# Reordering products in a Strassen feed-forward block: P2 behind the last pair's P4, another start, and P2 second in the second product

## The chip, the core and the metric

The kernel runs on one NeuronCore of one Trainium2 chip. The metric is device time in microseconds (us). A run is one launch of the whole kernel; the figure for a kernel is the median of its runs. TensorE (PE in the profile) multiplies matrices into PSUM, VectorE (DVE), ScalarE (ACT) and GpSimd (POOL) do the elementwise work, and SyncE (SP) issues the DMA transfers.

## What is computed

One decoder block on a sequence of 1024 tokens of width 1024, in float32. The change touches only the second half, the feed-forward part with 2 x 2816 hidden columns:

```python
def conv_ffn(h, w_up, conv_w, conv_b, w_down):
    u = causal_dwconv(h @ w_up, conv_w) + conv_b
    gate, val = jnp.split(u, 2, axis=-1)
    return (jax.nn.silu(gate) * val) @ w_down

x = layer_norm(ALPHA * x + (1.0 + gt_a) * y, ln1_g[l], ln1_b[l])
h = x * (1.0 + sc_f) + sh_f
y = conv_ffn(h, ffn_w_up[l], ffn_conv[l], ffn_conv_b[l], ffn_w_down[l])
x = layer_norm(ALPHA * x + (1.0 + gt_f) * y, ln2_g[l], ln2_b[l])
```

## The kernel before

**Precision.** Every float32 matrix is held as a high part and a rest ("hi" and "lo", in the names aH/aL, whi/wlo, vh/vl, s1l), and every block product is three matmuls: hi x lo, lo x hi, hi x hi.

**The first product, h @ w_up (lines 1281 to 1535).** It is a Strassen-Winograd scheme: the operands are split 2 x 2 (tokens and reduction on one side; reduction, and gate or value columns, on the other), and seven products P1 to P7 replace eight. The 2816 gate columns go in 22 blocks of 128, each with its block of value columns; one such block f is called a pair here. `product(f, i)` issues Pi of pair f: 12 matmuls of 128x512 at line 1281. A pair owns two PSUM tiles of two halves each: gp[f] holds P2 in half 0 and collects P1, P6, P7, P4 in half 1; vp[f] holds P5 and then P3 in half 0. Dependencies are tracked by whole tiles, so a matmul into one half waits for a reader of the other.

`carry(f, i)` does what must follow a product. After P1 ScalarE copies half 1 (L1471, the p1 copy), after P5 it copies vp (L1473), after P6 it copies the running sum (L1475). `add_p1` (L1458, VectorE) adds the p1 copy to P2's half. After P3 VectorE adds at L1479, after P7 at L1481. Then `conv` makes the causal convolution of 1024 tokens (ScalarE at L1400, two VectorE operations at L1403), first for the value block after P7, then for the gate block after P4, where silu (L1462) and the multiplication by the value block (L1463) follow. The sums that the second product needs are made and split at L1410 and L1411 and stored to DRAM buffers dS1 to dS7 (L1412, L1413, L1427, L1434) two pairs at a time.

`weights(f + 1)` makes the sums of weight blocks for the next pair on VectorE while a pair runs: L1333 (which waits for the weight load vq, issued at L1326), L1336, L1346, L1347, each split at L1305 and L1306. L157 and L158 split the raw weight block.

The order of TensorE's work is written out by hand (`manual_schedule`); the other engines' orders are made by a scheduler from the program text. Before, a pair runs as P2(f), P4(f-1), P6(f), P3(f), P7(f), P1(f+1), P5(f+1). The last pair has P4(f-1), P6, P3, P7, P2 and then P4.

**Where the first product begins (lines 1288 to 1385).** The last layer-norm rows are transposed (`h2_of(t)`), and sums of the left operand (s1 to s4, L1363) are made by VectorE while the first products run.

**The second product, (silu(gate) x val) @ w_down (lines 1545 to 1720).** Again seven products, each of 11 steps j with 4 row blocks t: 132 matmuls (L1634 to L1636). `ORDER` sets the order of the products; P4 comes last, row block by row block, its last one in two column halves. `entry(i, j)` loads an operand pair five steps ahead of TensorE into a ring of eight slots (L1611 to L1620): the left operand from dS, the right one from w_down, through `b_of`, which keeps some blocks in R0 and R1 and others in a ring of six buffers "bt". Two sets of PSUM banks take turns: on1 collects P1, P6, P7, P4; on5 takes P5, P3, P2. `collect` adds a finished product to the accumulators, and `ln2` normalises a row block and stores it. All loads are issued by SP in one queue.

Of the kernel before, what the change touches and what calls it, by code (L numbers as in the profile page):

```python
# [87 lines left out]
def build(ctx, tc, out, cst, x, c, ln0_g, ln0_b, w_ada, b_ada, w_in, dn_conv, dn_a_log, dn_dt_bias,  # L88
# [1198 lines left out]
    with tc.manual_schedule(engines={PE.engine}):  # L1287
        for t in range(NT):
            y_half(t, 1)
            ln1(t)  # L1290
            if t >= LAG:
                h2_of(t - LAG)
        raw = {0: gate_block(0), 1: gate_block(1)}
        product(0, 1)
        product(0, 2)
    mix.close()
    ffn1 = ExitStack()
    fp = ffn1.enter_context(tc.tile_pool(name="ffn1", bufs=1, reuse_waits="tile"))
# [66 lines left out]
    with tc.manual_schedule(engines={PE.engine}):  # L1365
        load_w(0)
        ahead = weights(0)
        next(ahead)
        next(ahead)
        h2_of(NT - 2)  # L1370
        product(1, 1)
        next(ahead)
        for i, tag in ((5, "s1"), (6, "s2"), (3, "s4"), (7, "s3")):
            hi = {5: aH[:, KH[0], HS[1]], 7: aL[:, KH[0], HS[1]]}.get(i)
            if hi is None:
                hi = ft([P, 4, 512], tag + "h", 1, F32R)
            parts_s[i] = hi, ft([P, 4, 512], tag + "l", 1, F32R)
            opA[i] = (lambda k, hl=parts_s[i]: tuple(a[:, :, ct(k)] for a in hl))
        h2_of(NT - 1)
        product(1, 2)  # L1380
        for i in (5, 6):
            for r0, r1 in ((0, 2), (2, 3), (3, 4)):
                split_last = s_rows(i, r0, r1)
        next(ahead, None)
        for i, rows in ((3, ((0, 4),)), (7, ((0, 3), (3, 4)))):
            for r0, r1 in rows:
                with tc.issue_after(split_last[0].ins), tc.issue_after(split_last[1].ins):
                    s_rows(i, r0, r1)
# [49 lines left out]
    def residual_rows(n):  # L1438

        hf, t = n // NT, n % NT  # L1440
        if t == 0:
            for box, v, tag in ((g1h, ln1_g, "g1h"), (b1h, ln1_b, "b1h")):
                box[0] = ft([P, 512], tag, 1)
                nc.sync.dma_start(box[0], v[0][HS[hf]].partition_broadcast(P))
                S.mul(box[0], box[0], ALPHA)
        r = r_cells[n % 2]
        d = ax2[t * P:(t + 1) * P, HS[hf]]
        nc.sync.dma_start(r, d)
        yield
        with tc.issue_after(anchor[0].ins):  # L1450
            V.tensor_tensor(r, r, g1h[0], op=ALU.mult)
            V.tensor_tensor(r, r, b1h[0], op=ALU.add)
        nc.sync.dma_start(d, r)

    pending, anchor = [], [None]

    def add_p1(f):
        V.tensor_tensor(gp[f][:, 0, :], gp[f][:, 0, :], p1_, op=ALU.add)  # L1458
# [8 lines left out]
    def carry(f, i):  # L1467

        g, v = gp[f], vp.get(f)
        if i == 1:  # L1470
            S.copy(p1_, g[:, 1, :])  # L1471
        elif i == 5:
            S.copy(p5_, v[:, 0, :])  # L1473
        elif i == 6:
            S.copy(u2_, g[:, 1, :])  # L1475
        elif i == 2 and f < NF - 1:
            add_p1(f)
        elif i == 3:
            anchor[0] = V.tensor_tensor(v[:, 0, :], v[:, 0, :], u2_, op=ALU.add)  # L1479
        elif i == 7:  # L1480
            V.tensor_tensor(v[:, 1, :], g[:, 1, :], p5_, op=ALU.add)  # L1481
            if f == 0:
                V.tensor_tensor(g[:, 1, :], g[:, 1, :], p4_, op=ALU.add)
            conv(g_row(f), NF + f, v)
            if f == 0:
                gate_end(f)
        elif i == 4 and f:
            if f == NF - 1:
                add_p1(f)
            gate_end(f)  # L1490
# [8 lines left out]
    with tc.manual_schedule(engines={PE.engine}):  # L1499
        product(0, 4)  # L1500
        S.copy(p4_, vp[0][:, 1, :])
        for f, i in ((0, 1), (0, 2), (1, 1), (1, 2)):
            carry(f, i)
        load_w(1)
        ahead = weights(1)
        next(ahead)
        for i in (5, 6, 3, 7):
            step(0, i)
            if i != 5:
                next(ahead, None)  # L1510
        for f in range(1, NF):
            more = f + 1 < NF
            if f == 1:
                seq = (5, 6, 3, 7)
            elif more:
                seq = (2, -4, 6, 3, 7)
            else:
                seq = (-4, 6, 3, 7, 2)
            if more:
                load_w(f + 1)  # L1520
                ahead = weights(f + 1)
            for i in seq:
                step(*((f, i) if i > 0 else (f - 1, -i)))
                if i == (5 if f == 1 else -4):
                    split_q(f, 4, wq[f])
                    if more:
                        next(ahead)
                    if 4 <= f < 4 + 2 * NT:
                        pending.append(residual_rows(f - 4))
                elif i in (6, 3, 7) and more:  # L1530
                    next(ahead, None)
            if more:
                step(f + 1, 1)
                step(f + 1, 5)
        step(NF - 1, 4)
        while pending:
            for _ in pending.pop(0):
                pass
# [18 lines left out]
    ln2_rows = []  # L1557
    stat2 = dt_([P, NT, 4, 6], "stat2")
    R0 = fr.tile([P, NJ, 512], F32, tag="R0", name="R0")
    ORDER = (1, 5, 6, 3, 7, 2, 4)  # L1560
    SPARE = (NJ - 3, NJ - 2, NJ - 1)
    ents, spare2 = {}, []
    R1_ = []
# [4 lines left out]
    def b_of(i, j):  # L1568

        r0, r1 = R0[:, j, :], R1_[0][:, j, :] if R1_ else None  # L1570
        if i in (6, 3):
            b = dt_([P, 512], "bt", 6)
            load_b(b, j, 1, 1)
            if i == 3:
                return b
            V.tensor_tensor(r1, b, r1, op=ALU.subtract)
            return r1
        if i == 1:
            load_b(r0, j, 0, 0)
        elif i == 2:  # L1580
            load_b(r0, j, 1, 0)
        elif i == 5:
            load_b(r1, j, 0, 1)
            V.tensor_tensor(r1, r1, r0, op=ALU.subtract)
            return r1
        elif i == 7:
            V.tensor_tensor(r0, r1, r0, op=ALU.subtract)
        else:
            V.tensor_tensor(r0, r0, r1, op=ALU.subtract)
        return r0  # L1590

# [83 lines left out]
    def collect(i, t, pb):  # L1675
        if i == 1:
            S.copy(c11(t), pb)
        elif i == 5:
            S.copy(c22(t), pb)
        elif i == 6:  # L1680
            S.copy(c12(t), pb)
        elif i == 3:
            done(c12(t), pb, HS[1], res[t, 1], c12(t))
            stats(t, HS[1], 512)
        elif i == 7:
            done(c22(t), pb, HS[1], res[t + 4, 1], c22(t))
            stats(t + 4, HS[1], 512 if t < 3 else 256)
        elif i == 2:
            done(c11(t), pb, HS[0], res[t, 0], c11(t))
            stats(t, HS[0], 512)  # L1690
            ln2(t, 2, CUT_EARLY)

    steps = [(i, j) for i in ORDER for j in range(NJ)]
    AHEAD = 5
    with tc.manual_schedule(engines={PE.engine}):
        n = AHEAD
        for s in steps[:AHEAD]:
            entry(*s)
        nc.sync.dma_start(gate, dG5.partition_broadcast(P))
        two = lambda: [b[:, h, :] for b in (bank2(0), bank2(1)) for h in range(2)]  # L1700
        on1, on5 = two(), two()
        for i in ORDER[:-1]:
            pbs = on5 if i in (5, 3, 2) else on1
            for j in range(NJ):
                if n < len(steps):
                    entry(*steps[n])
                    n += 1
                if i == 3 and j == 0:
                    ln2_rows.extend(rows_of(2, ln2_g[0], ln2_b[0]))
                if j == 4:  # L1710
                    for t in range(4):
                        if i in (3, 7, 2):
                            residual(t + 4 if i == 7 else t, 0 if i == 2 else 1)
                for t in range(4):
                    matmuls(pbs[t], i, j, t)
            for t in range(4):
                collect(i, t, pbs[t])
        while n < len(steps):
            entry(*steps[n])
            n += 1  # L1720
        for t in range(4):
            residual(t + 4, 0)
        for t in (0, 2, 1, 3):
            for sl in (HS[0],) if t < 3 else (slice(0, 256), slice(256, 512)):
                for j in range(NJ):
                    matmuls(on1[t][:, sl], 4, j, t, sl)
                done(acc[:, t + 4, sl], on1[t][:, sl], sl, res[t + 4, 0][:, sl])
                stats(t + 4, sl, 512 if t < 3 else 256)
            ln2(t + 4, 2 if t < 3 else 4, CUT_EARLY if t < 3 else CUT)
# [21 lines left out]
```

## Time and profile before

| | us |
|---|---|
| median of 3 runs (1445.4 to 1447.4) | 1446.18 |
| the profiled execution's own time | 1447.39 |
| its span in the profile | 1445.7 |

Busy over the span, from the page: PE 1337.2 us (92%), DVE 1005.0 (70%), ACT 590.1 (41%), POOL 532.9 (37%). The first product runs from about 745 to 1215 us of the span, the second from there to the end.

The page gives the totals; the trace behind it can be asked for a stretch of time. A windows view gives busy time, granted TensorE clock (1.00 is full speed) and DMA share by stretch; a waits view sums the time an engine sat idle, by the line that waited and what released it; a timeline gives single instructions, with the idle time before each in brackets; a lines view groups instructions by line and shape.

### The profile page before, as it was taken

What the parts mean: (1) busy time and instruction counts of PE and PEld (TensorE: products, weight loads), DVE (VectorE), ACT (ScalarE), POOL (GpSimd) and SP (SyncE); (2) the same over time, 40 slices, a digit from 0 to 9 for tenths busy, and PEclk for the clock granted to TensorE, in tenths of its full rate; (3) what the DMA queues carried; (4) which work ended last, traced back from release to release, by engine and by line L of the source; (5) the groups of instructions that cost most, each with busy time, mean ns of one, the idle gap of its engine ahead of it and who ended that gap; (6) DMA issues with size and microseconds to landing.
All of it is one profiled execution on the core that took longest, in us unless ns stands there. A gap on an engine that the chain in (4) does not pass through costs nothing.

```text
span 1445.7 us, 19012 instructions
## 1 busy us (share of the span) xinstructions
PE 1337.2 (92%) x6662; PEld 1061.9 (73%) x6662; DVE 1005.0 (70%) x1770; ACT 590.1 (41%) x957; POOL 532.9 (37%) x369
## 2 busy tenths in 40 slices
PE   6796999999999899999988989999899998999995
PEld 4564768787887678777866767777687786788885
DVE  7885955487547432794497768877988887732777
ACT  4356222233234332352565444454544544353222
POOL 2674311122115667352323433444444331342006
PEclk9898999999999999899999999999999998999998
DMA  9557212122203464253132343445444438975773
GB/s 316 148 157 208 65 32 59 32 68 57 58 23 102 139 190 146 88 189 117 78 113 80 103 140 126 143 160 189 148 143 160 153 119 307 391 243 162 266 252 117
DMA packets 195572, 209.15 MB, mean 145 GB/s; under 512 B 30099, under 2 KB 125199, under 8 KB 195477
## 3 DMA queue, kind: packets, MB, share of 16 engines
q1 hardware_dynamic: 195189, 206.89, 44.5%
q8 instruction: 53, 0.87, 0.3%
q10 hardware_dynamic: 288, 1.05, 0.2%
q14 instruction: 42, 0.34, 0.1%
HBM read 149.92 MB, written 57.97 MB: 144 GB/s over the span
## 4 chain that ended last, share of the span: by engine, by line
PE 50%; DVE 23%; DMA 10%; issue 9%; POOL 4%; ACT 3%; SPq 1%; POOLq 0%; DVEq 0%; ACTq 0%
PE up L1281 9%; PE pp L622 6%; PE pp L623 5%; PE pp L624 5%; PE up L1634 4%; PE up L1636 4%; PE up L1635 4%; DMA vq<-in_ffn_w_up 3%; DVE ob L1403 2%; DVE vq L1333 1%; POOL vl L1306 1%; PE dn L864 1%; DVE mac L236 1%; DMA K<-in_w_ada 1%; DVE vl L1306 1%
## 5 line engine op out<-in xcount | busy, mean ns | idle before, releaser
L622 PE MATMUL pp<-aH,wlo 128*128 128x512 f32 x432 | 190.9, 442 | 8.8 <-DVE ob L651 6.4
L158 POOL TENSOR_TENSOR wlo<-wst,whi 128x1024 fp32r<-128x1024 f32 x50 | 122.6, 2452 | 160.0 <-ACT whi L157 159.5
L624 PE MATMUL pp<-aH,whi 128*128 128x512 f32 x432 | 176.8, 409 | 0.0
L623 PE MATMUL pp<-aL,whi 128*128 128x512 f32 x432 | 176.7, 409 | 0.0
L1306 POOL TENSOR_TENSOR vl<-vq,vh 128x512 fp32r<-128x512 f32 x44 | 70.2, 1595 | 213.3 <-ACT vh L1305 209.0
L1634 PE MATMUL up<-aL,aH 128*128 128x512 f32 (+1 forms) x304 | 118.7, 391 | 11.8 <-DVE ob L1669 7.1
L1403 DVE SCALAR_TENSOR_TENSOR ob<-up,colC,ob 128x1023 f32<-128x1023 f32 (+1 forms) x88 | 112.2, 1276 | 20.8 <-ACT ob L1400 19.5
L1635 PE MATMUL up<-aH,aL 128*128 128x512 f32 (+1 forms) x304 | 118.2, 389 | 0.0
L1636 PE MATMUL up<-aH 128*128 128x512 f32 (+1 forms) x304 | 118.2, 389 | 0.0
L622 PEld LDWEIGHTS pp<-aH,wlo 128*128 128x128 f32 x432 | 85.0, 197 | 30.7 <-DVE ob L651 5.1
L624 PEld LDWEIGHTS pp<-aH,whi 128*128 128x128 f32 x432 | 84.9, 196 | 20.6
L623 PEld LDWEIGHTS pp<-aL,whi 128*128 128x128 f32 x432 | 85.5, 198 | 14.5 <-issue 0.5
L1281 PE MATMUL up<-aH,wlo 128*128 128x512 f32 x176 | 74.0, 420 | 17.4 <-ACT ob L1471 14.1
L157 ACT CAST whi<-wst 128x1024 fp32r<-128x1024 f32 x50 | 52.3, 1046 | 82.6 <-DMA wst<-in_ffn_w_up 31.5
L1616 ACT CAST aH<-R 128x512 fp32r<-128x512 f32 x63 | 39.1, 621 | 100.7 <-PE up L1636 94.1
L1617 DVE TENSOR_TENSOR aL<-R,aH 128x512 fp32r<-128x512 f32 x63 | 44.1, 705 | 51.9 <-ACT aH L1616 51.8
L1634 PEld LDWEIGHTS up<-aL,aH 128*128 128x128 f32 x304 | 58.5, 192 | 24.5 <-DVE ob L1669 7.3
L1281 PE MATMUL up<-aH,vl 128*128 128x512 f32 x176 | 70.8, 402 | 5.8 <-DVE vl L1306 4.2
L1281 PE MATMUL up<-aH,whi 128*128 128x512 f32 x176 | 71.9, 409 | 0.0
L1281 PE MATMUL up<-aL,whi 128*128 128x512 f32 x176 | 71.7, 407 | 0.0
L1281 PE MATMUL up<-aL,vh 128*128 128x512 f32 x176 | 70.4, 400 | 0.0
L1281 PE MATMUL up<-aH,vh 128*128 128x512 f32 x176 | 70.1, 398 | 0.0
(520 smaller groups left out, 3395.6 us busy)
## 6 DMA issues: line engine op xcount, KB each, us to landing
wst<-in_w_in SPq DMA_DIRECT2D x28, 512.0 KB
K<-in_w_ada SPq DMA_DIRECT2D x48, 256.0 KB, 3.0
wst<-in_ffn_w_up SPq DMA_DIRECT2D x22, 512.0 KB
vq<-in_ffn_w_up SPq DMA_DIRECT2D x44, 256.0 KB, 3.1
R<-in_ffn_w_down SPq DMA_DIRECT2D x33, 256.0 KB, 5.4
wada<-in_w_ada SPq DMA_DIRECT2D x8, 1024.0 KB, 8.8
dS<-ob SPq DMA_DIRECT2D x22, 256.0 KB, 2.4
st<-dS SPq DMA_DIRECT2D x22, 256.0 KB, 3.9
```

The source lines that it names most:

```text
L157: S.copy(hi, st)
L158: eng.tensor_tensor(lo, st, hi.bitcast(F32), op=ALU.subtract)
L622: PE.matmul(pp, lo[:, k, :], aH[:, k, sl], start=(k == 0), stop=False)
L623: PE.matmul(pp, hi[:, k, :], aL[:, k, sl], start=False, stop=False)
L624: PE.matmul(pp, hi[:, k, :], aH[:, k, sl], start=False, stop=(k == NK - 1))
L1281: PE.matmul(o, w[:, k, :], a, start=flags[0], stop=flags[1], skip_group_check=not first_)
L1306: eng.tensor_tensor(lo, q, hi.bitcast(F32), op=ALU.subtract)
L1403: V.scalar_tensor_tensor(t[:, sh:], cb[:, :T - sh], w(j), t[:, sh:], op0=ALU.mult, op1=ALU.add)
L1617: V.tensor_tensor(lo[:, HS[1]], b, hi[:, HS[1]].bitcast(F32), op=ALU.subtract)
L1634: PE.matmul(pb, l_hi, r_lo, start=new, stop=False, skip_group_check=i not in (1, 5, 2))
L1635: PE.matmul(pb, l_lo, r_hi, start=False, stop=False, skip_group_check=i not in (1, 5, 2))
L1636: PE.matmul(pb, l_hi, r_hi, start=False, stop=(j == NJ - 1), skip_group_check=i not in (1, 5, 2))
```

## The change

Five edits. (1) Where the first product begins, the transposes of row block 6 come ahead of P1 of pair 0, and P2 of pair 0 comes after the transposes of row block 7. (2) The scaling of two layer-norm vectors on ScalarE is issued after the p5 copy. (3) `add_p1` of a pair from 2 on is issued after P3 instead of after P2. (4) In pairs 2 to 20, P4 of the last pair comes ahead of P2. (5) In the second product P2 is the second product instead of the sixth; its right operand goes through the ring of six, so P4 loads those blocks again (11 loads of 256 KB more); the first half of the final normalisation moves from P2's collect to P3's.

```diff
@@ the first product begins
                 h2_of(t - LAG)
+        h2_of(NT - 2)
         raw = {0: gate_block(0), 1: gate_block(1)}
         product(0, 1)
-        product(0, 2)
...
-        h2_of(NT - 2)
         product(1, 1)
...
         h2_of(NT - 1)
+        product(0, 2)
         product(1, 2)
@@ residual_rows
-                S.mul(box[0], box[0], ALPHA)
+                with tc.issue_after(anchor[1].ins):
+                    S.mul(box[0], box[0], ALPHA)
@@ carry
         elif i == 5:
-            S.copy(p5_, v[:, 0, :])
+            anchor[1] = S.copy(p5_, v[:, 0, :])
...
-        elif i == 2 and f < NF - 1:
+        elif i == 2 and f < 2:
             add_p1(f)
         elif i == 3:
             anchor[0] = V.tensor_tensor(v[:, 0, :], v[:, 0, :], u2_, op=ALU.add)
+            if 2 <= f < NF - 1:
+                add_p1(f)
@@ the order of a pair
             elif more:
-                seq = (2, -4, 6, 3, 7)
+                seq = (-4, 2, 6, 3, 7)
@@ the second product
-    ORDER = (1, 5, 6, 3, 7, 2, 4)
+    ORDER = (1, 2, 5, 6, 3, 7, 4)
...
-        if i in (6, 3):
+        if i in (6, 3, 2):
             b = dt_([P, 512], "bt", 6)
-            load_b(b, j, 1, 1)
-            if i == 3:
+            load_b(b, j, 1, int(i != 2))
+            if i != 6:
                 return b
...
-        elif i == 2:
-            load_b(r0, j, 1, 0)
...
         else:
+            load_b(r0, j, 1, 0)
             V.tensor_tensor(r0, r0, r1, op=ALU.subtract)
...
         elif i == 3:
             done(c12(t), pb, HS[1], res[t, 1], c12(t))
             stats(t, HS[1], 512)
+            ln2(t, 2, CUT_EARLY)
...
         elif i == 2:
             done(c11(t), pb, HS[0], res[t, 0], c11(t))
             stats(t, HS[0], 512)
-            ln2(t, 2, CUT_EARLY)
...
-                if j == 4:
+                if j == (0 if i == 2 else 4):
```

Two places show how the change moves instructions. The first is VectorE's order within one late pair of the first product, where "up" is a PSUM tile (gp or vp), vq and wst are weights, and ob is a row in SBUF. Before:

```order
L1333 TENSOR_TENSOR vq_9365<-vq_9365,wst_9369 128x512 [waits DMAHW5_49,DMAHW2_49,Pool_49]
L1458 TENSOR_TENSOR up_9193<-up_9193,ob 128x512 [waits PE_49]
L1403 SCALAR_TENSOR_TENSOR ob<-up_9035,colC,ob 128x1023 [waits Activation_49]
L1306 TENSOR_TENSOR vl_9273<-vq_9227,vh_9272 128x512 [waits Activation_49]
L1403 SCALAR_TENSOR_TENSOR ob<-up_9035,colC,ob 128x1022 [waits DVE_49]
L1433 TENSOR_TENSOR ob<-ob 128x512 [waits Pool_49]
L1336 TENSOR_TENSOR vq_9227<-vq_9228,vq_9227 128x512 [waits DMAHW7_49,DVE_49]
L1479 TENSOR_TENSOR up_9211<-up_9211,ob 128x512 [waits PE_49,Activation_49]
```

After:

```order
L1333 TENSOR_TENSOR vq_9365<-vq_9365,wst_9369 128x512 [waits DMAHW6_49,DMAHW3_49,Pool_49]
L1433 TENSOR_TENSOR ob<-ob 128x512 [waits Activation_49,Pool_49]
L1403 SCALAR_TENSOR_TENSOR ob<-up_9035,colC,ob 128x1023 [waits Activation_49]
L1306 TENSOR_TENSOR vl_9260<-vq_9227,vh_9259 128x512 [waits Activation_49]
L1403 SCALAR_TENSOR_TENSOR ob<-up_9035,colC,ob 128x1022 [waits DVE_49]
L1336 TENSOR_TENSOR vq_9227<-vq_9228,vq_9227 128x512 [waits DMAHW2_49,DVE_49]
L1346 TENSOR_TENSOR ob<-wst_9231,vq_9227 128x512 [waits DVE_49]
L1464 TENSOR_TENSOR ob<-ob 128x1024 [waits Activation_49]
L1459 TENSOR_TENSOR up_9197<-up_9197,ob 128x512 [waits Activation_49]
L1306 TENSOR_TENSOR vl_9294<-vq_9227,vh_9293 128x512 [waits Activation_49]
L1480 TENSOR_TENSOR up_9213<-up_9213,ob 128x512 [waits PE_49]
```

`add_p1` (L1458 before, L1459 after) moved from second place behind L1333 to behind the gate's multiplication (L1464, which was L1463), still ahead of L1480 (which was L1479).

The second place is SP's queue in the second product, where the last entry of the product that runs second is loaded. Before (the product is P5, its operands dS5h and dS5l):

```order
L1614 DMA aL<-dS5l 128x512
L1613 DMA aH<-dS5h 128x512
L1566 DMA bt_10249<-in_ffn_w_down 128x512
L1566 DMA bt_10269<-in_ffn_w_down 128x512
L1611 DMA st_10101<-dS_6408 128x512
```

After (the product is P2, its operands dS2h and dS2l):

```order
L1616 DMA aL<-dS5l 128x512
L1615 DMA aH<-dS5h 128x512
L1569 DMA bt_10388<-in_ffn_w_down 128x512
L1615 DMA aH<-dS2h 128x512
L1569 DMA bt_10409<-in_ffn_w_down 128x512
L1569 DMA bt_10430<-in_ffn_w_down 128x512
L1701 DMA gate<-dG_825 128x1024
L1616 DMA aL<-dS2l 128x512
L1615 DMA aH<-dS5h 128x512
```

Counted from the first load of dS1, the last load of dS5h before is the 110th DMA of the queue; the last load of dS2l after is the 132nd, behind six pairs of dS5 loads (for the product after it) and the gate load, which before was the 120th.

## Rows read from the trace of the kernel before

**Rows 1.** The windows view: engines' busy us, granted clock, DMA share, GB/s.

```profile
728.00:767.00 39.00, 29.71 (x120) 22.56 (x119) 38.28 (x57) 25.19 (x44) 9.09 (x5) 0.87 0.27 85
...
787.00:850.00 63.00, 55.28 (x217) 43.44 (x216) 43.73 (x46) 28.21 (x40) 23.35 (x14) 0.92 0.34 109
850.00:1200.00 350.00, 335.65 (x1428) 269.37 (x1427) 292.50 (x318) 171.46 (x246) 153.01 (x93) 0.99 0.46 154
...
1215.00:1275.00 60.00, 59.33 (x249) 48.32 (x250) 46.62 (x67) 23.48 (x40) 18.17 (x8) 0.96 1.05 390
1275.00:1398.00 123.00, 123.00 (x545) 101.83 (x544) 59.69 (x94) 42.49 (x73) 22.04 (x17) 1.00 0.68 226
1398.00:1446.00 48.00, 32.61 (x167) 28.10 (x165) 39.85 (x71) 10.22 (x18) 22.96 (x16) 0.89 0.35 123
```

**Rows 2.** The waits view of PE from 780 us: total us, times, longest.

```profile
PE up L1281 <- ACT ob L1471: 14.1, 8, 2.5
PE up L1634 <- DVE ob L1669: 7.1, 1, 7.1
PE up L1281 <- DVE up L1458: 6.5, 3, 3.2
```

**Rows 3.** The timeline of ACT behind a P7: start, duration, instruction.

```profile
939.23 1.20 ACT L1400 ACTIVATE ob<-up,colC 128x1024 f32<-128x1024 f32 x1 [1.20 <-DVE up L1481]
940.33 0.57 ACT L1471 COPY ob<-up 128x512 f32<-128x512 f32 x1
```

**Rows 4.** The timeline of PE: the first matmul of P2, two pairs apart.

```profile
940.96 0.50 PE L1281 MATMUL up<-aH,wlo 128*128 128x512 f32 x1 [1.65 <-ACT ob L1471]
...
982.29 0.50 PE L1281 MATMUL up<-aH,wlo 128*128 128x512 f32 x1 [2.18 <-ACT ob L1471]
```

**Rows 5.** The windows view around clock falls and the second product's start.

```profile
841.00:848.00 7.00, 5.63 (x13) 4.51 (x14) 5.59 (x7) 0.12 (x2) 0.16 (x1) 0.53 0.00 0
1214.88:1220.00 5.12, 5.12 (x12) 4.06 (x13) 5.12 (x7) 3.73 (x6) 0.00 (x0) 0.50 1.05 396
1220.00:1247.00 27.00, 27.00 (x120) 22.29 (x120) 21.88 (x36) 8.97 (x15) 9.34 (x2) 0.99 1.05 392
1247.00:1275.00 28.00, 27.33 (x120) 22.09 (x119) 19.74 (x26) 10.89 (x19) 8.83 (x6) 1.00 1.04 387
```

**Rows 6.** The waits view of PE from 728 to 790 us.

```profile
PE up L1281 <- DVE vl L1306: 4.2, 1, 4.2
```

**Rows 7.** The lines view, 850 to 1200 us: VectorE's groups in a pair, busy us, mean ns.

```profile
L1403 DVE SCALAR_TENSOR_TENSOR ob<-up,colC,ob 128x1023 f32<-128x1023 f32 x34 | 43.5, 1279 | 15.4 <-ACT ob L1400 14.6
...
L1463 DVE TENSOR_TENSOR ob<-ob 128x1024 f32<-128x1024 f32 x18 | 31.5, 1748 | 0.0
L1306 DVE TENSOR_TENSOR vl<-vq,vh 128x512 fp32r<-128x512 f32 x33 | 30.1, 911 | 0.0
...
L1333 DVE TENSOR_TENSOR vq<-vq,wst 128x512 f32<-128x512 f32 x15 | 26.7, 1780 | 35.3 <-DMA vq<-in_ffn_w_up 31.8 <-POOL vl L1306 2.3 <-POOL gate L1411 1.2
...
L1346 DVE TENSOR_TENSOR ob<-wst,vq 128x512 f32<-128x512 f32 x16 | 19.8, 1238 | 0.8
```

**Rows 8.** The timeline of DVE in two pairs.

```profile
948.42 0.94 DVE L1333 TENSOR_TENSOR vq<-vq,wst 128x512 f32<-128x512 f32 x1 [2.68 <-DMA vq<-in_ffn_w_up]
...
961.08 0.68 DVE L1347 TENSOR_TENSOR vq<-vq,wst 128x512 f32<-128x512 f32 x1
...
968.38 2.53 DVE L1333 TENSOR_TENSOR vq<-vq,wst 128x512 f32<-128x512 f32 x1 [3.32 <-DMA vq<-in_ffn_w_up]
```

**Rows 9.** The timeline of POOL in the second of these pairs.

```profile
967.96 2.39 POOL L158 TENSOR_TENSOR wlo<-wst,whi 128x1024 fp32r<-128x1024 f32 x1 [2.91 <-ACT whi L157]
```

**Rows 10.** The timeline of SP's queue: last load of P5's operands, gate load.

```profile
1267.63 0.32 SPq L1613 DMA_DIRECT2D aH<-dS5h  x1
...
1273.91 0.32 SPq L1699 DMA_DIRECT2D gate<-dG  x1
```

**Rows 11.** DMA issues from 1215 to 1275 us: KB, median us to landing.

```profile
aH<-dS5h SPq DMA_DIRECT2D x11, 256.0 KB, 5.2
```

More of the change, by code (lines that the diff above doesn't have):

```diff
@@ L1453, in residual_rows @@
         nc.sync.dma_start(d, r)
-    pending, anchor = [], [None]
+    pending, anchor = [], [None, None]
     def add_p1(f):
```

## The prediction

> **What bounds the kernel now.** I read the windows view by stage first, then the waits of TensorE (PE), then the timelines of one pair, then the queue of loads.
>
> In the first product TensorE has the most work: 335.65 of 350.00 us between 850 and 1200 us, against 292.50 on VectorE [rows 1]. A matmul costs 335.65 / 1428 = 0.235 us there, so a product of 12 takes 2.82 us and a pair of seven 19.74. The first matmuls of P2 two pairs apart lie 982.29 - 940.96 = 41.33 us apart [rows 4], 20.67 a pair: 0.9 us a pair is lost. The waits say where: 14.1 us for the p1 copy (L1471), which P2 waits for, and 6.5 us for add_p1 (L1458), which P6 waits for [rows 2]. Behind a P7 the copy stands after the convolution of the value block on ScalarE: 939.23 to 940.43, then the copy to 940.90 [rows 3], and P2 starts at 940.96, 1.65 us late [rows 4].
>
> Around 728 to 767 us the bound is VectorE, 38.28 of 39.00 us busy [rows 1], and TensorE waits 4.2 us for one of its results [rows 6]. In the second product TensorE is busy throughout, but until 1275 us the DMA engines are saturated too: share 1.05, 390 GB/s [rows 1]. At the end TensorE waits 7.1 us for L1669 on VectorE [rows 2], which has 39.85 us of work in the last 48 [rows 1].
>
> The granted clock has two levels. It falls to half (1.2 of 2.4 GHz) around a long wait: from 841 to 848 us 13 matmuls ran, 13 x 0.235 = 3.1 us worth, with 5.63 us busy [rows 5], so that fall cost 2.6 us beside its wait.
>
> **The change, part by part**, against the profiled execution's own time of 1447.39 us, which lies 1.2 above the median of 1446.18.
>
> *Where the first product begins.* TensorE's order changes; VectorE's work does not, and it ends the stage. Taking the nearest wait as the size [rows 6], the change could give 4.2 us back or add as much. The transposes now come before product work that could have run, while VectorE's list stays as long, so I take **+1**.
>
> *The scaling of two vectors, issued behind a p5 copy.* It happens twice in the kernel and is hidden by the product that runs beside it: 0. If that cover is gone it delays one p1 copy, which is a wait already counted.
>
> *The pairs, what is lost now.* From 850 to 1200 us TensorE is idle 350.00 - 335.65 = 14.4 us, and a mean clock of 0.99 costs another 350 x 0.01 = 3.5. From 787 to 850 us 217 matmuls need 51.0 of 63.00 us [rows 1]: 12.0 lost. Together 30 us. With P4(f-1) in front, the p1 copy has 2.82 us more; its waits were at most 2.5 us [rows 2], so they go. The wait of P6 for add_p1 goes as well. At the start of the stage about 3 us stay, because the weight loads there set the pace, not the copy.
>
> *The pairs, what is new.* add_p1 is now behind the gate's multiplication on VectorE, and P7 waits for it. What else is late behind it: L1480, then L1347, and with it the next weight load. Count from P4's start: P4 ends at 2.82, the gate's convolution on ScalarE (1.20, [rows 3]) at 4.0. Then VectorE does two L1403 (1.28 each), L1306, L1336, L1346, the multiplication and add_p1. Unstretched that is 2.56 + four operations of 0.7 + 1.2 = 6.6, and add_p1 ends at 10.6; P7 starts at 4 x 2.82 = 11.3, so no wait. With the mean durations (L1306 0.91, L1346 1.24, the multiplication 1.75 [rows 7], two of 0.7) it ends at 11.9: a wait of 0.6. The load does not forbid this: L1347 to the next L1333 took 968.38 - 961.08 = 7.3 us [rows 8], and L1347 now follows P3's end, 8.5 us before P4's start; so L1333 starts within a microsecond of P4's start and is done, even at 2.53 us, before the convolution ends.
>
> The durations on VectorE depend on GpSimd: the same L1333 took 0.94 us at one place and 2.53 at another [rows 8], where it began 0.42 us into L158 on GpSimd (967.96, 2.39 long [rows 9]) and ended 0.56 after it. If one operation ahead of add_p1 is held for the whole of such an instruction, add_p1 ends 2.4 later than unstretched, and P7 waits 10.6 + 2.4 - 11.3 = 1.7 us.
>
> The Trainium skill (SBUF — State Buffer, section "SBUF: two separate sides") says that VectorE and GpSimd share one port pair under an exclusive lock: an operation on VectorE with two SBUF inputs waits for the whole GpSimd instruction, rather than sharing. The two rows agree with it, 0.56 us being about one unhindered operation. By that rule a pair that meets L158 ahead of add_p1 has a wait of 1.7 us and one that doesn't has none, so the pairs would lie at one of the two ends below.
>
> I take 0.55 us a pair, for 18 pairs 10 us, with 0 and 1.7 as ends. Pairs: 30 - 3 - 10 = **-17** (from -27 to +4).
>
> *P2 second in the second product.* Its left operands arrive in the queue where P5's did, except the last. P1's 132 matmuls end at 1247.0 (12 by 1220, 120 more by 1247 [rows 5]). Ten of the eleven steps of the next product take 27.0 us (120 matmuls, as P1's 120 did), so entry 10 is needed at 1274.0. Before, its load was the 110th of the queue, issued at 1267.63 [rows 10], landing 5.2 us later [rows 11]: in time. Now it is the 132nd. From the 110th to the gate load, the 120th, the queue took 1273.91 - 1267.63 = 6.28 us [rows 10], 0.63 each. 22 more, the gate's counted double, are 23 x 0.63 = 14.5 us: issue at 1282.1, landing at 1287.3, 13.3 us late. The other end: if only slots of the ring bind, the load of entry 5 of P5 in front waits for step 8 of P2, at 1247.0 + 9 x 12 x 0.225 = 1271.3; seven more units of 0.63 and 5.2 to land give 1280.9, 6.9 late. With the DMA saturated I take 12, and 2 for the clock that falls with it (2.6 for the fall above): **+14**.
>
> *P2 then P5 on the same banks.* P5 waits until VectorE has read them. One operation (0.7) before the first is free, or up to seven (4.8) if collects and operand sums are in front. VectorE has caught up during the stall: **+1**.
>
> *Half of the final normalisation in P7's time.* VectorE had 59.69 us in 123, 14.6 in a product of 30; at most half of the 39.85 us of the last stretch joins [rows 1]: 34.5 us in 30. P4, on the same banks, starts 0 to 4.4 us late: **+2**.
>
> *The end.* Without that work in P4's time the 7.1 us wait [rows 2] and its clock fall go, but the collect of the last halves stays: 4 to 8.5 us, taken as **-6**. The 11 added loads fall in a stretch with DMA share 0.68 [rows 1] and cost nothing there; without that room each would cost 0.63.
>
> Sum: 1 - 17 + 14 + 1 + 2 - 6 = -5, so 1442.4 on the profiled execution, and **1441** on the median.
>
> **The rivals.**
>
> *P7's wait takes the place of P2's.* If VectorE is held in most pairs ahead of add_p1, as L1333 was behind L158 [rows 8, 9], the mean wait w is over 0.55 us. The total is -15 + 18 x w, so it turns slower at w = 0.83 us a pair. At 1.2 us it is +7, 1453 us; at 1.7, +16, 1462. For it: VectorE's means are already stretched (1.75 for 1.22). Against: the longest stretches lie where GpSimd splits weights (L158), which is early in the pair. 0.22.
>
> *The entry comes in time.* If SP's queue runs ahead because P1 and the stores leave it room, the 14 us vanish: 1427. For it: loads can be issued as soon as a slot is free. Against: the DMA share of 1.05 while P1 runs. 0.15.
>
> *The pair change does not do what it says.* P4 moves to the place where VectorE's L1481 has just freed its operands (ScalarE's next step began at 939.23 [rows 3], P2 could have started at 939.3). If VectorE is 1 us later there, P4 waits in P2's place, and only the start of the stage gains, 8 us: 1450. 0.11.
>
> *The forecast*: 0.52, alone 1433 to 1449, from the ends of its late entry, its end and the wait at P7.
>
> **How the numbers follow.** A measurement can tell this kernel from no change by about 0.2%, 2.9 us: faster is below 1443.3, slower above 1449.1. Faster: 0.82 of the forecast and the second rival, 0.43 + 0.15 = 0.58. Same: 0.08 of the forecast, 0.05 of the third, 0.03 of the first rival: 0.16. Slower: 0.26. The range, 1425 to 1455, holds the forecast, the second and third rival and the milder half of the first; it leaves out some 0.15.
>
> **What would show it.** Right: no wait for the p1 copy in pairs from 3 on; waits at P7 for add_p1 of 0 to 1 us; a period near 20.2 us; one wait of about 12 us in P2's last step; no wait for L1669 at the end. Wrong: a period of 20.7 or more, with P7 waiting; no stall in P2's time; or a second stall between P2 and P5, or P7 and P4, of over 4 us.

## The result and the profile after

| | before | after |
|---|---|---|
| median of the runs, us | 1445.79 (1442.8 to 1447.4, 4 runs) | 1495.65 (1489.73 to 1497.36, 4 runs) |
| the profiled execution's own time | 1447.39 | 1494.28 |
| its span | 1445.7 | 1492.6 |

The ratio is 1.034, with a 95% interval from 1.0306 to 1.0374: the change makes the kernel slower by 3.4%, 50 us, where 5 us less were forecast and 1455 was the upper end.

The waits view of PE from 780 us, of the kernel after, answers to [rows 2]:

```profile
PE up L1281 <- DVE up L1459: 44.4, 18, 5.4
PE up L1636 <- DMA aH<-dS2h: 12.5, 2, 11.5
PE up L1636 <- DVE ob L1673: 7.4, 2, 6.7
PE up L1636 <- issue: 3.5, 1, 3.5
PE up L1637 <- DMA aL<-dS2l: 2.7, 1, 2.7
PE up L1281 <- DVE up L1484: 1.9, 2, 1.7
```

The p1 copy's waits are gone, as forecast (none of L1472 is left), and so is the wait of 7.1 us at the end. In their place P7 waits in each of 18 pairs for add_p1 (L1459), 2.47 us on average; before, the copy and add_p1 together cost 20.6 us.

The windows view answers to [rows 1]; the second product begins 28 us later than before, so only the first two lines stand against the same stretch of [rows 1], and the second of them holds less of the work:

```profile
787.00:850.00 63.00, 53.76 (x216) 42.60 (x216) 47.22 (x48) 29.79 (x43) 22.32 (x14) 0.92 0.37 117
850.00:1200.00 350.00, 314.82 (x1290) 250.42 (x1291) 278.81 (x295) 159.12 (x226) 140.32 (x86) 0.96 0.43 141
...
1243.00:1300.00 57.00, 56.27 (x240) 46.14 (x240) 36.40 (x52) 20.58 (x35) 3.86 (x3) 0.97 1.05 386
1300.00:1326.00 26.00, 10.41 (x33) 7.51 (x34) 11.77 (x19) 2.55 (x5) 0.00 (x0) 0.67 0.84 309
```

In the same 350 us TensorE did 1290 matmuls instead of 1428, at a mean clock of 0.96 instead of 0.99. From 1300 to 1326 us, the end of P2 in the second product, it did 33 matmuls, worth 33 x 0.225 = 7.4 us, in 26.

The timeline of PE shows the two kinds of wait at P7, which take turns (apart from the first pair, 5.4 us, and one of 3.9):

```profile
917.04 0.76 PE L1281 MATMUL up<-aL,vl 128*128 128x512 f32 x1 [3.07 <-DVE up L1459]
...
939.40 0.47 PE L1281 MATMUL up<-aL,vl 128*128 128x512 f32 x1 [1.34 <-DVE up L1459]
...
962.15 0.47 PE L1281 MATMUL up<-aL,vl 128*128 128x512 f32 x1 [3.05 <-DVE up L1459]
```

Two pairs take 962.15 - 917.04 = 45.1 us, 22.6 a pair, against 20.67 before [rows 4]. Where the 46.9 us between the two profiled executions went: the second product starts at 1243.25 instead of 1214.88, 28.4 later; from there to the end of the span it takes 249.4 us instead of 230.8, 18.5 more.

What delays add_p1 in the pair with 3.05 us is seen in the timeline of DVE, from the gate's convolution on (P4 had ended and ScalarE's part, L1400, ran from 950.92 to 952.13):

```profile
950.22 0.69 DVE L1333 TENSOR_TENSOR vq<-vq,wst 128x512 f32<-128x512 f32 x1 [0.34 <-DMA vq<-in_ffn_w_up]
953.84 0.69 DVE L1433 TENSOR_TENSOR ob<-ob 128x512 f32<-128x512 f32 x1 [2.93 <-POOL ob L1411]
954.45 1.28 DVE L1403 SCALAR_TENSOR_TENSOR ob<-up,colC,ob 128x1023 f32<-128x1023 f32 x1
955.65 2.09 DVE L1306 TENSOR_TENSOR vl<-vq,vh 128x512 fp32r<-128x512 f32 x1
957.66 1.27 DVE L1403 SCALAR_TENSOR_TENSOR ob<-up,colC,ob 128x1022 f32<-128x1022 f32 x1
...
960.17 1.22 DVE L1464 TENSOR_TENSOR ob<-ob 128x1024 f32<-128x1024 f32 x1
961.31 0.69 DVE L1459 TENSOR_TENSOR up<-up,ob 128x512 f32<-128x512 f32 x1
```

and of POOL beside it:

```profile
952.52 1.29 POOL L1411 TENSOR_TENSOR ob<-ob 128x512 fp32r<-128x512 f32 x1
954.79 2.40 POOL L158 TENSOR_TENSOR wlo<-wst,whi 128x1024 fp32r<-128x1024 f32 x1 [0.98 <-ACT whi L157]
```

The gate's L1403 was ready at 952.13 and started at 954.45, because L1433 (a12 - a11, a sum for the second product, made once in two pairs) stood ahead of it and waited for GpSimd. Then L1306 took 2.09 us, ending 0.55 after L158 on GpSimd. The pair with 1.34 us has no such sum, but meets L158 as well, in the timelines of DVE and of POOL:

```profile
934.12 2.59 DVE L1336 TENSOR_TENSOR vq<-vq,vq 128x512 f32<-128x512 f32 x1
```

```profile
933.76 2.41 POOL L158 TENSOR_TENSOR wlo<-wst,whi 128x1024 fp32r<-128x1024 f32 x1 [3.85 <-ACT whi L157]
```

So it is in all 18 pairs: L158 runs ahead of add_p1, and one operation on VectorE (mostly L1306 or L1336) ends 0.54 to 0.56 us after it. L1433 stands ahead of add_p1 in nine of the pairs, each with a wait of 3.0 us or more. The tenth long wait, in the first pair, has a late weight load (4.06 us at L1333) in its place. The waits view of DVE from 850 to 1190 us has eight of the nine:

```profile
DVE ob L1433 <- POOL ob L1411: 11.4, 4, 2.9
DVE ob L1433 <- POOL gate L1411: 8.7, 4, 2.8
```

This is a loop: P7, P1, P5 and P4 follow each other on TensorE; P4 starts the gate's convolution; add_p1 stands behind all of that on VectorE; and the next P7 waits for add_p1. Between P4's end and P7's start TensorE has P2, P6 and P3 to do, three products or 8.5 us. Whatever the chain takes beyond that is lost in every pair and can't be caught up.

### The profile page after: what moved, and what is told of

It is laid out like the page before. It is cut to its first block, busy times and chain, and to the rows that moved or that the text cites. A ratio compares the mean times of both kernels' runs of the same rounds, so it can differ in the third digit from the quotient of the medians.

```text
span 1492.6 us, 18953 instructions
## 1 busy us (share of the span) xinstructions
PE 1345.8 (90%) x6662; PEld 1065.5 (71%) x6662; DVE 1013.1 (68%) x1770; ACT 591.7 (40%) x957; POOL 522.0 (35%) x369
## 4 chain that ended last, share of the span: by engine, by line
PE 51%; DVE 25%; DMA 12%; issue 5%; ACT 3%; POOL 3%; SPq 1%; POOLq 0%; DVEq 0%; ACTq 0%
PE up L1281 10%; PE pp L622 6%; PE pp L623 5%; PE pp L624 5%; DVE ob L1403 3%; PE up L1636 3%; PE up L1637 3%; PE up L1638 3%; DVE vq L1336 2%; DMA R<-in_ffn_w_down 2%; DMA bt<-in_ffn_w_down 2%; DMA dS5h<-gate 1%; DVE ob L1464 1%; PE pp L1182 1%; PE pp L1183 1%
## 5 line engine op out<-in xcount | busy, mean ns | idle before, releaser
L158 POOL TENSOR_TENSOR wlo<-wst,whi 128x1024 fp32r<-128x1024 f32 x50 | 121.4, 2430 | 187.7 <-ACT whi L157 187.2
L1403 DVE SCALAR_TENSOR_TENSOR ob<-up,colC,ob 128x1023 f32<-128x1023 f32 (+1 forms) x88 | 112.3, 1278 | 40.9 <-ACT ob L1400 40.0
L1306 POOL TENSOR_TENSOR vl<-vq,vh 128x512 fp32r<-128x512 f32 x44 | 64.5, 1466 | 183.6 <-ACT vh L1305 183.6
L157 ACT CAST whi<-wst 128x1024 fp32r<-128x1024 f32 x50 | 52.5, 1050 | 82.0 <-PE pp L624 30.7
L1305 ACT CAST vh<-vq 128x512 fp32r<-128x512 f32 x89 | 54.8, 618 | 75.4 <-PE up L1281 38.5
L1281 PE MATMUL up<-aL,vl 128*128 128x512 f32 x88 | 42.4, 482 | 44.4 <-DVE up L1459 44.4
L1281 PE MATMUL up<-aL,vh 128*128 128x512 f32 x176 | 75.9, 431 | 0.0
L1281 PE MATMUL up<-aH,wlo 128*128 128x512 f32 x176 | 70.5, 401 | 1.7 <-DVE up L1484 1.7
```

Source lines behind the costliest of these rows:

```text
L157: S.copy(hi, st)
L158: eng.tensor_tensor(lo, st, hi.bitcast(F32), op=ALU.subtract)
L1281: PE.matmul(o, w[:, k, :], a, start=flags[0], stop=flags[1], skip_group_check=not first_)
L1305: S.copy(hi, q)
L1306: eng.tensor_tensor(lo, q, hi.bitcast(F32), op=ALU.subtract)
L1403: V.scalar_tensor_tensor(t[:, sh:], cb[:, :T - sh], w(j), t[:, sh:], op0=ALU.mult, op1=ALU.add)
```

## The experiments

Theory A: the loop just named. Its rivals are named with each run. Each kernel is compared with runs of the kernel before on the same chip, whose median stands beside it.

### The halves of the change

**pairs_only**: the kernel before with the pair order and add_p1's place alone.

```diff
-        elif i == 2 and f < NF - 1:
+        elif i == 2 and f < 2:
             add_p1(f)
...
+            if 2 <= f < NF - 1:
+                add_p1(f)
...
-                seq = (2, -4, 6, 3, 7)
+                seq = (-4, 2, 6, 3, 7)
```

> The kernel before with edits 3 and 4 alone (P4 of the last pair ahead of P2, add_p1 behind P3). Theory A, P7's wait for add_p1 closes a loop P7, P1, P5, P4, convolution, gate multiplication, add_p1, P7 that is longer than a pair's products: P7 waits in 18 pairs, about 44 us in all, a period of 22.5 us, and the second product begins some 28 us later than in the kernel before: about 1474 us. Rival B, the loss comes from the second product and from what its loads do to the stage before: about 1446 us, P7's waits below 10 us in all.

Measured: 1468.75 us against 1445.32, ratio 1.0171 (1.0144 to 1.0198). P7 waits 39.9 us in 18 pairs, 1.3 and 3.0 in turns. The second product starts at 1237.95 us, 23.1 later than before, where 28 were expected. The pairs alone cost 23 us; rival B falls.

**second_only**: the kernel before with the second product's edit alone (`ORDER = (1, 2, 5, 6, 3, 7, 4)` and what goes with it).

> The kernel before with edit 5 alone (P2 second in the second product). Theory A, the two halves of the change add: the last entry of P2 comes 11 to 14 us late, P4 starts 4 to 7 us late behind P7, the end gains 5 to 6: about 1446 + 18 = 1464 us. Rival B, the entry is late only because the slower pairs store dS2 late: a stall below 5 us, about 1450 us.

Measured: 1459.32 us, ratio 1.0097 (1.0067 to 1.0127): 14 us. P2's last entry comes 4.7 + 4.2 us late and P4 waits 6.3. The two halves make 37 of the 50 us. In the profiled executions the whole change loses 5.3 us more ahead of the second product than pairs_only, and 5.1 more in it than second_only; the executions of one kernel spread (1439.6 to 1452.8 us for the kernel before), and what adds this was not tested. With the pairs as before the entry's wait is smaller, though not below 5 us: 9.7 us of waits for P2's operands against 15.2 in the whole change. So most of the delay belongs to the second product's edit, and it is larger in the whole change: between the theories.

**start_only**: the new order where the first product begins, alone.

> The kernel before with edit 1 alone (the order where the first product begins). VectorE's work there stays the same: the time stays within 3 us of the kernel before. If the new order leaves VectorE idle at the transposes, up to 4 us slower; if its waits on TensorE's side go, up to 4 us faster.

Measured: 1445.93 us against 1444.93, ratio 1.0016 (0.9998 to 1.0035): no difference that this measurement can tell.

**p4_first_only**: P4 ahead of P2, add_p1 still behind P2.

> The kernel before with edit 4 alone: P4 of the last pair ahead of P2, add_p1 still behind P2, so that P6 waits for it. Theory A: add_p1 now stands behind one convolution step of the gate, 4 us behind P4's end, while P6 is due 2.8 us behind it: P6 waits 1.2 us or more in each pair, the copy's waits go: 1445 to 1460 us. Rival G, putting P4 first is by itself worth the copy's waits: 1430 to 1438 us.

Measured: 1472.59 us against 1444.93, ratio 1.0201 (1.0166 to 1.0236), slower than expected by either. The waits are at P6 instead of P7 and as large in sum, 1.0 to 1.1 and 2.0 to 5.1 us in turns:

```profile
PE up L1281 <- DVE up L1458: 41.1, 19, 5.1
```

Here add_p1 stands on VectorE behind the gate's first L1403 and an L1306, ahead of the multiplication. So it is not add_p1's place behind the gate's multiplication alone that costs: with P4 ahead of P2, add_p1 follows a step of the gate's convolution on VectorE in either kernel, and P6 or P7 waits for it. Which of the two places is better is not shown: the intervals of the two ratios overlap.

### What stands in the loop

A table of two by two takes apart what stands ahead of add_p1. It is not quite clean: in the two kernels with the multiplication behind it, add_p1 is issued after P6 instead of after P3, and the sums for the second product start two products later. **pairs_mul_late** puts the gate's multiplication behind add_p1:

```diff
...
+                a = add_p1(f)
+                with tc.issue_after(a.ins):
+                    gate_mul(f - 1)
```

> As pairs_only, but the gate's multiplication (1.2 us on VectorE) is issued behind add_p1 instead of ahead of it; every engine's work stays the same. Theory A: each wait of P7 falls by 1.2 us, to about 0.1 and 1.9 in turns, 18 us in all instead of 44, fewer clock falls, and the time is some 22 to 28 us below pairs_only, 1446 to 1452 us. Rival C, the period is set by VectorE's round of weight sums (load, L1333 to L1347, next load), to which the multiplication belongs wherever it stands: no change against pairs_only within 5 us, P7 or another product waits for something else.

**pairs_only_sum_late** puts L1433 behind it:

```diff
         put_split(2, j, a12, G)
-        yield
-        V.tensor_tensor(a12, a12, a11, op=ALU.subtract)
+        for _ in range(6):
+            yield
+        with tc.issue_after((anchor[2] or anchor[0]).ins):
+            V.tensor_tensor(a12, a12, a11, op=ALU.subtract)
```

> As pairs_only, but the sum a12 - a11 (L1433 of the kernel before) is queued on VectorE behind add_p1 of the next pair, instead of ahead of the gate's convolution. Theory A2, in every second pair VectorE stands at this sum, which waits for GpSimd, and the gate's chain stands behind it: the waits of 3.05 us at P7 fall to about 1.3, those of 1.3 stay, P7 waits some 24 us in all instead of 40; with the clock falls that go, 20 to 30 us below pairs_only, 1440 to 1450 us. Rival F, the long waits come from GpSimd's L158 holding VectorE, not from the sum: the waits stay near 3 us, the time stays near 1469.

In this kernel the sum for the last block but one is made after its row has been written again, so P3's operand of that block has other values; the work is the same.

**pairs_sum_late** does both (with 3 instead of 6).

> As pairs_mul_late, with the sum a12 - a11 also behind add_p1. Theory A2: both reasons for P7's wait are gone, P7 waits below 5 us in all, a period of 19.8 to 20.2 us a pair, and the time is 1422 to 1432 us, below the kernel before. Rival C, VectorE's round of weight sums sets the period at 20.7 us or more: 1440 us or more, another wait in P7's place.

The waits are those of one execution each.

| ahead of add_p1 | us | ratio to before | P7 waits, us |
|---|---|---|---|
| both (pairs_only) | 1468.75 | 1.0171 (1.0144 to 1.0198) | 39.9 |
| the sum (pairs_mul_late) | 1461.44 | 1.011 (1.008 to 1.014) | 31.6 |
| the multiplication (pairs_only_sum_late) | 1442.37 | 0.9992 (0.9972 to 1.0012) | 27.3 |
| neither (pairs_sum_late) | 1433.86 | 0.9929 (0.9907 to 0.995) | 17.6 |

Here are the waits and the window from 850 to 1150 us, of pairs_only_sum_late:

```profile
PE up L1281 <- DVE up L1460: 27.3, 18, 3.4
```

```profile
850.00:1150.00 300.00, 280.09 (x1197) 223.31 (x1196) 255.67 (x270) 146.53 (x209) 131.39 (x79) 1.00 0.46 153
```

and the same window of pairs_only:

```profile
850.00:1150.00 300.00, 270.27 (x1112) 215.07 (x1111) 236.74 (x251) 137.08 (x196) 119.02 (x74) 0.96 0.44 146
```

With the sum out of the way 16 of the 18 waits are 1.3 us (the others 3.4, in the first pair, and 2.6), as theory A2 had it, and rival F falls: 12.6 us less of waits, and 26 us less of time. L158 still holds an operation in the pairs with 1.3 us (L1336 takes 2.59 us at 921.21), so it is in the short waits and not in the difference. The rest of the 26 us goes with the clock: 1.00 instead of 0.96 over the stretch, 1197 matmuls instead of 1112. In pairs_only the granted clock over the 7 us behind a wait was 1.00 for each of the nine waits of 1.3 us, and 0.56 to 0.80 for seven of the nine of 3 us.

The multiplication behaves otherwise. In pairs_mul_late the waits of 1.3 us fell to 0.2, but the others grew to between 3.3 and 4.1 (the first excepted, 2.3). In six of these nine pairs L1433 now fell between the two steps of the convolution, waited for GpSimd there, and was then held itself, in the pair shown until 0.55 us behind L158, in the timeline of DVE and of POOL:

```profile
944.57 1.28 DVE L1403 SCALAR_TENSOR_TENSOR ob<-up,colC,ob 128x1023 f32<-128x1023 f32 x1 [0.93 <-ACT ob L1400]
946.74 2.86 DVE L1433 TENSOR_TENSOR ob<-ob 128x512 f32<-128x512 f32 x1 [0.89 <-POOL ob L1411]
```

```profile
946.66 2.39 POOL L158 TENSOR_TENSOR wlo<-wst,whi 128x1024 fp32r<-128x1024 f32 x1
```

So it gained 7 us where 22 to 28 were expected: rival C's "no change" is wrong, and theory A's size was. A fix in the loop is worth little while another instruction can take the place.

**pairs_sum_late** beats both kernels: 0.7% below the kernel before, though 2 us above what was expected. P7 waits 17.6 us instead of the 5 expected, 0.6 to 2.9 in eleven of the pairs and 0.2 in the others.

**pairs_add_first** was to remove that rest: the weight sums L1336 and L1346 are also queued behind add_p1.

```diff
+        if anchor[3]:
+            with tc.issue_after(anchor[3].ins):
+                V.tensor_tensor(B12, B22, B12, op=ALU.subtract)
...
```

> As pairs_sum_late (1434 us, P7 still waiting 17.6 us), but the weight sums L1336 and L1346 of the kernel before are queued behind add_p1 too, so that add_p1 follows the gate's convolution directly on VectorE. Theory A: add_p1 ends some 5 to 6 us behind P4's end, before P7 is due at 8.5; P7's waits fall below 4 us in all, the time to 1420 to 1427 us. Rival C, VectorE's round of weight sums now sets the period, because L1336 and L1346 come later and the next weight load with them: another wait appears, at P6 or P3 of the next pair or at the weights, and the time stays at 1432 us or more.

Measured: 1463.47 us against 1444.49, ratio 1.013 (1.0094 to 1.0166). It failed. The waits are still P7's for add_p1, 29.9 us in 12 pairs, by two ways. In six of them, with 15.9 us, L1334 (L1333 of the kernel before) stands on VectorE ahead of the gate's convolution (L1408 here) and waits for its weight load, in the timeline of DVE:

```profile
879.83 2.50 DVE L1334 TENSOR_TENSOR vq<-vq,wst 128x512 f32<-128x512 f32 x1 [4.97 <-DMA vq<-in_ffn_w_up]
882.26 1.27 DVE L1408 SCALAR_TENSOR_TENSOR ob<-up,colC,ob 128x1023 f32<-128x1023 f32 x1
```

P7 then starts at 887.82, 4.11 us late. ScalarE's part of that convolution was done at 876.7, so the weights held the chain. In each of these six pairs add_p1 then waits 1.66 us more for ScalarE's copy after P6 (L1487), which stands behind silu, so it does not follow the convolution directly as the edit meant it to. The late weight load and the time above 1432 us are what rival C had, though the wait shows at P7 and not at a place that it named; why the load is late was not taken apart. In the other six pairs, with 14.0 us, the chain begins late because the gate's convolution (L1405 here) stands on ScalarE behind a cast that waits for a store, in the timeline of ACT:

```profile
944.72 0.62 ACT L1415 CAST ob<-ob 128x512 fp32r<-128x512 f32 x1 [3.87 <-DMA dS5h<-ob]
945.24 1.21 ACT L1405 ACTIVATE ob<-up,colC 128x1024 f32<-128x1024 f32 x1
```

P2's first matmul had started at 940.93, so P4 was done at 941.1 and 4 us of the 8.5 were gone before the convolution started. The scheduler made a new order on ScalarE around the shifted sums. Which of the two ways costs more of the time is not separated by a run. **pairs_add_first_mul**, with the scaling of the two vectors moved as well, is the same within its interval:

> As pairs_add_first, with edit 2 (the scaling of the two vectors behind a p5 copy). It happens twice: 0 to 3 us below pairs_add_first, by the one wait of 2.9 us at P7 near 990 us in pairs_sum_late; if that wait came from elsewhere, no difference.

Measured: 1461.15 us, ratio 1.0122 (1.0101 to 1.0144). The move of the scaling is worth nothing that can be told here.

### The second product

**second_put2**: as second_only, with dS2 stored ahead of dS5 and dS7.

```diff
+        put_split(2, j, a12, G)
+        yield
         put_split(5, j, a22, G)
...
         put_split(7, j, a21, G)
-        yield
-        put_split(2, j, a12, G)
```

> As second_only, but the parts for P2 (dS2) are stored ahead of those for P5 and P7 in every second pair; the bytes are the same. In the queue of loads P2's last entry moves from place 129 to place 112. Theory D, the stall is the place in the queue behind the late store: it falls from 11 to 14 us to below 2, and the time to some 13 us below second_only, about 1451 us. Rival E, the added loads fill the DMA engines, whatever the order: the same bytes must land before P2 ends, the stall stays above 9 us.

Measured: 1452.48 us against 1445.32, ratio 1.0064 (1.0031 to 1.0098). The waits for P2's operands fell from 9.7 us to 1.8, in the waits view:

```profile
PE up L1633 <- DVE ob L1670: 7.1, 2, 6.5
...
PE up L1633 <- DMA aH<-dS2h: 1.8, 2, 0.9
```

From its first matmul (1215.67) to the end of the span (1449.7) the second product takes 234.0 us; in second_only it was 1456.2 - 1211.95 = 244.3, in the kernel before 230.8. The bytes are the same; the late store and the place in the queue behind it, which moved together, were the cause, and rival E falls. What is left, 6.5 us before P4 against 7.1 at the end before, cancels: P2 second gains nothing.

**second_put2_ln2_late**: the normalisation written behind P7's collect.

> As second_put2, but the first half of the final normalisation is written behind P7's collect instead of P3's. If the 6.5 us before P4 are VectorE's normalisation in front of P7's collect, they fall below 2 us, and the wait of 7.1 us before P4's last half, which edit 5 had taken away, is back: the time within 3 us of second_put2. If the wait before P4 is the change of banks itself, it stays and the time is 7 us longer.

Measured: 1456.57 us against 1444.49, ratio 1.0081 (1.0056 to 1.0107). P4 still waits 5.6 us, and the wait of 7.1 us at the end is not back. Its second product takes 231.1 us in the profiled execution, not longer than second_put2's; the added time lies ahead of it, where the text of the two kernels is the same. This is inconclusive: the scheduler put the rows of the normalisation ahead of the collect again, so the edit did not make the order that it was to test. That the normalisation causes the wait is argued from the timeline (it fills VectorE up to the collect), not shown.

**all_loop_open**: all five edits, with the sums, the multiplication and the weight sums behind add_p1 and dS2 stored first.

> The whole change, with the loop opened: add_p1 ahead of the gate's multiplication and of the weight sums, a12 - a11 behind them, dS2 stored ahead of dS5. Theory A with D: the pairs as in pairs_add_first, the second product as in second_put2, which was 3 us longer than before's: 1424 to 1432 us, some 65 us below the change as it was. If what was lost lies elsewhere in the change, it stays above 1440.

Measured: 1451.17 us against 1444.49, ratio 1.0054 (1.0035 to 1.0073). So 43 of the 50 us are back, and 6.7 are left. The expected time was missed by 19 us, and by the expectation's other branch, above 1440, part of the loss lies elsewhere. In part it is in the pairs still: P7 waits 23.0 us in 8 pairs, and in seven of them L1334 had waited 2.6 to 5.6 us for the weight load, as in half of those of pairs_add_first; a cast waits for a store only once there, 1.3 us. Its second product takes 1446.9 - 1214.43 = 232.5 us, 1.7 more than before's. All five edits together with pairs_sum_late's order, without the move of the weight sums, were not run.

## Why the prediction was wrong

**The step that failed** is the term "the pairs, what is new": add_p1 was to end at 11.9 us from P4's start, 0.6 behind the 11.3 at which P7 is due, and 0.55 us a pair was taken, with 1.7 as the upper end. It measured 2.47 on average. The pairs with 1.34 lie inside these ends, the pairs with 3.05 and the average above them. Two things were wrong in its working.

- The sum L1433. The order quoted ahead of the prediction has it between L1333 and the gate's first L1403, waiting for GpSimd; the chain was counted without it. It goes with the difference between 1.34 and 3.05 us in every second pair, and its removal brought 26 us (pairs_only_sum_late).
- The mean durations. They came from the trace of before, where L158 on GpSimd ran at L1333 [rows 8, 9], and the first rival was held back because L158 is early in the pair. The change moves P2, which reads the weights that L158 writes, so L158 moved too: it waits for L157 on ScalarE, which waited for TensorE 14 times from 850 to 1190 us in the kernel after (13.8 us) and mostly for its load before. In all 18 pairs it ran inside the chain. So the upper end of 1.7, worked out for one operation held by L158, was the case of every pair, and the pairs without the sum measured 1.34.

The Trainium skill (SBUF — State Buffer, "SBUF: two separate sides") says that an operation on VectorE with two SBUF inputs is blocked for the whole of a GpSimd instruction that started first. The rows agree with it: L1336 and L1306 began 0.36 and 0.86 us into L158 and took 2.59 and 2.09 us, where L1333 and L1433, of the same shape, took 0.69.

**The price of a wait** was counted in this term as the wait alone. Between pairs_only and pairs_only_sum_late 12.6 us of waits were 26 us of time. Start and pairs were to bring the second product 16 us forward, and it came 28.4 later. That is 44.4 us apart. 18 x 0.55 = 9.9 us of waits at P7 were counted and 18 x 2.47 = 44.4 came, 34.5 more; the other 10 go with the clock, as far as the trace tells: in the 7 us behind eight of the ten longer waits the granted clock was 0.56 to 0.79, and TensorE did 176 matmuls there instead of 240, at 0.235 us each 15 us.

The gain that was taken at the start of the stage, 12.0 us lost there down to 3, did not come either: from 787 to 850 us TensorE did 216 matmuls, 217 before. Two of P7's waits, 5.4 and 3.1 us, lie in that stretch.

**The first rival** was this mechanism, with a chance of 0.22: at w = 2.47 its total, -15 + 18 x w, is +29. The measured difference of 46.9 is that, 7.5 for the second product (18.5 instead of the 11 that the sum had) and the 10 that go with the clock. The prediction's signs of being wrong came: a period of 22.6 us with P7 waiting, and a stall of over 4 us between P7 and P4.

**What was right.** P2's wait for the copy went. The start was worth +1 by forecast and nothing measurable alone. P2's last entry was forecast 12 us late, and TensorE waited 11.5 us for its first half, then 2.7 more for the second, in the timeline of PE:

```profile
1315.05 0.77 PE L1636 MATMUL up<-aL,aH 128*128 128x512 f32 x1 [11.52 <-DMA aH<-dS2h]
1318.55 0.77 PE L1637 MATMUL up<-aH,aL 128*128 128x512 f32 x1 [2.73 <-DMA aL<-dS2l]
...
1450.72 0.79 PE L1636 MATMUL up<-aL,aH 128*128 128x512 f32 x1 [6.66 <-DVE ob L1673]
```

From the first matmul of P1 to the first behind P2 it is 79.8 us, before to the first behind P5 63.7: with the clock fall the term measured 16 instead of 14. The load is the 132nd of the queue as counted, and was issued 13 us behind its store, in the timeline of SP:

```profile
1299.11 0.32 SPq L1413 DMA_DIRECT2D dS2l<-gate  x1
...
1312.29 0.33 SPq L1616 DMA_DIRECT2D aL<-dS2l  x1
```

P2 then P5 on the same banks was +1 and measured 0.79. The end was -6; the wait of 7.1 us is gone, and from P4's first matmul to the end of the span it is 41.9 us instead of 47.5. P4 behind P7 was +2 with an upper end of 4.4, and measured 6.66 (the last row above): mis-sized, and with the entry most of the 7.5 us.

**The second rival** (the entry in time) would have needed the store earlier, as second_put2 shows. **The third** (VectorE late at P4's start) did not happen: P4 follows P5 without a wait.

## What to carry to other kernels

When a step is moved ahead, follow what its result starts on the other engines, in their order, until it comes back: if that chain closes on the same engine, its length, and not the waits that are removed, sets the period. Count every instruction that stands in the chain in the new order, those that wait for a third engine first of all, and take durations from where they will run, not their mean from where they ran. And a wait behind which the clock falls costs more than its length: 12.6 us of waits were 26 us of time here, and waits of 1.3 us had no such price.

## What was unexpected

Equal waits did not always have the same price. In the kernel after, P7 at 917.04 came behind a wait of 3.07 us and P7 at 962.15 behind one of 3.05, and the windows behind them differ:

```profile
917.00:924.00 7.00, 6.96 (x24) 5.62 (x25) 5.52 (x8) 2.33 (x3) 2.57 (x2) 0.79 0.61 173
939.40:946.40 7.00, 7.00 (x30) 5.69 (x31) 6.97 (x10) 3.41 (x6) 4.54 (x3) 1.00 0.59 189
962.00:969.00 7.00, 6.85 (x30) 5.58 (x31) 5.72 (x9) 2.92 (x5) 2.60 (x2) 1.00 0.57 171
```

The granted clock fell to its lower level, 1.2 GHz, for part of the first window (24 matmuls in 7 us instead of 30) and not at all in the third. In the kernel after, eight of the ten waits of 3 us or more were followed by a fall and none of the eight of 1.3 us; but in the kernel before, the wait of 2.0 us ahead of the matmul at 789.81 was followed by one too (0.76 over 7 us). No run here tells what decides it.
